# A third buffer for loaded weight units paid for with two 4 KB tiles, and three joining copies queued behind the last weight cast

## The chip, the core and the metric

The kernel runs on one core of a Trainium2 chip. The metric is the time of one execution on the device in microseconds (us), lower is better. The kernel before takes 910.29 us, the median of three runs (908.7 to 912.39).

A core has engines that work side by side, each with its own queue in which instructions start in order: TensorE (PE in the profile, with its weight loads as PEld), VectorE (DVE), ScalarE (ACT), GpSimd (POOL) and SyncE (SP). SP computes nothing here; its queue issues the DMAs that bring weights from memory. An instruction that waits for a semaphore holds up all that stands behind it in its queue.

## The reference, cut to what matters

Two layers of an encoder on a sequence of 256 tokens with 1024 columns, all in float32:

```
u = rms_norm(h) ;  one projection u @ w_in -> parts of both branches
branch A (gated linear attention), branch B (grouped-query attention)
mixed = sigmoid(gate_A) * A + sigmoid(gate_B) * B
h = h + rms_norm(mixed @ w_out)
gate, up = split(rms_norm(h) @ w_ffn_in)          # FFN, 2 x 2816 columns
h = h + rms_norm((silu(gate) * up) @ w_ffn_out)
h = h + rms_norm(sigmoid(h @ w_ple_gate) * (p @ w_ple_proj))
```

With 256 tokens every weight is used once for two blocks ("halves", `hf` 0 and 1) of 128 tokens, so the whole of the weights, 169.50 MB read from memory in the profile, passes through the core in one execution.

## The kernel before, in words

**Three products for one.** TensorE multiplies operands that are rounded to a shorter float format. To keep float32's precision each operand is held as a high part (the rounded value) and a low part (what the rounding lost), and a product is taken as high x high, high x low and low x high. `split` (line 133) makes both parts: a copy with a cast on ACT gives the high part, a subtraction on DVE the low part. Both are recorded at line 135, for weights and for activations.

**Weight units.** The weights are cut into units of up to 128 x 2112 floats (8448 bytes on each of 128 partitions). `plan` lists them in the order of use. `Stream` carries them: `start` (line 290) takes a buffer of the pool `rawp` (tiles `raw`, two buffers) and issues the load on SP's queue (line 298); `put` takes a pair of tiles `wh` and `wl` from `wp` (four buffers each); `fill` (line 347) traces the two halves of the unit's split, two casts of 128 x 1024 on ACT and two subtractions on DVE, and then calls `load`, which traces the next load. At most `depth` units (3 or 4) are held cast and unused.

**Seven products for eight.** Some blocks of the gate stage and of the FFN (`PAIRS`) go through `seven` (line 711), which forms sums of weight units and of activations, and does with seven products of 128 x 512 x 512 what takes eight otherwise. `step` (line 323) makes the sums of weights on DVE (lines 327, 330, 333, 338: 128 x 2048 each); the units involved are loaded into borrowed `wh` and `wl` buffers (tiles `lent`) and into a large tile (`big`).

**Order of the FFN.** The string `FFN` (line 43) is the order written by hand: `u` is a step of a plain block (`block`), a digit a step of `seven`, `o` a step of the output product for one unit of `w_ffn_out` (`out_step`, whose matmuls are recorded at line 107; those of the other products at line 123), `p` a load of a gain vector. The blocks are finished in the order of `OUT`.

**Turning the hidden values.** After `silu(gate) * up` a tile of hidden values must be transposed. `turned` (line 1580) does it for all but the last pair by DMA: `turn_out` (line 456) lets ACT part the 32-bit words into two planes of 16 bits (lines 461 and 466) and issues a transposing DMA on SP's queue (line 467); some steps later `take_in` (line 470) lets ACT join the planes again (line 474, the "joining copy", 128 x 1024 elements of 16 bits) and splits the result into the tile `hid`, again with ACT and DVE. The gate stage uses the same pair of functions for the gated output of branch A (line 1467). The last pair of the FFN is transposed on TensorE instead.

**How instructions are ordered.** The program is traced once. Then a scheduler plays it through with estimated durations: on each engine it issues the earliest traced instruction whose operands and buffer are ready in that play, and a tile is given a buffer of its pool when one is free. The order it finds is fixed in the engines' queues. `tc.issue_after(ins)` adds an edge: what is traced within it on the engine of `ins` is queued behind `ins`, without waiting for its end. `tc.high_priority` moves instructions ahead in that choice.

**Buffers.** `b4p` holds ten tiles of 4096 bytes per partition (`mid`) for gains, sums, parted planes and other things; `smp` holds small ones, `rstd` (1 column) and `hss` (8 columns) with four buffers each.

The lines that the change touches are the pools (74 and 77), `Stream` (259, 319 to 321, 347 to 354), `take_in` (470 to 478), `row_rstd` (509), `last_norm` (619), `outputs` (1383) and `turned` (1580 to 1595).

Of the kernel before, what the change touches and what calls it, by code (L numbers as in the profile page):

```python
# [43 lines left out]
PLAIN, PAIRS = (4, 5, 10), (2, 6, 8)  # L44
# [17 lines left out]
def trunk_kernel(ctx: ExitStack, tc: tile.TileContext, a: dict, out: bass.AP):  # L62
# [8 lines left out]
    PSUM = bass.MemoryType.PSUM  # L71

    cp = ctx.enter_context(tc.tile_pool(name="cp", bufs=1))
    rawp = ctx.enter_context(tc.tile_pool(name="rawp", bufs=2))
    wp = ctx.enter_context(tc.tile_pool(name="wp", bufs=4))
    bigp = ctx.enter_context(tc.tile_pool(name="bigp", bufs=9))
    b4p = ctx.enter_context(tc.tile_pool(name="b4p", bufs=10))
    smp = ctx.enter_context(tc.tile_pool(name="smp", bufs=4))
    accp = ctx.enter_context(tc.tile_pool(name="accp", bufs=8, space=PSUM))

# [167 lines left out]
    class Stream:  # L248
# [7 lines left out]

        def __init__(self, depth):
            self.depth, self.held, self.room, self.ready, self.open = depth, 0, 0, [], False
            self.loads, self.jobs, self.lend, self.last = [], [], False, {}
            pairs = {}  # L260
            for item in plan:
                if callable(item):
                    x = Load(item)
                    self.loads.append(x)
                    self.jobs.append(lambda x=x: self.plain(x))
                else:
                    units, n = item
                    if n == 1:
                        b11, b12, b21, b22 = units
                        x, z = (Load(b, lambda tag=tag: self.lent(tag), tag == "wh") for b, tag in ((b11, "wh"), (b12, "wl")))  # L270
                        y, q = Load(b22, big), Load(b21)
                        pairs[id(units)] = x, y, z, q
                        self.loads += [x, y, z]
                    if n == 5:
                        self.loads.append(q)
                    self.jobs.append(lambda p=pairs[id(units)], n=n: self.step(n, *p))
# [41 lines left out]

        def made(self, x):
            for piece in self.put(x):  # L320
                split(*piece)

        def step(self, n, x, y, z, q):
            c = slice(0, 2048)
# [22 lines left out]
        def fill(self):  # L347
            while self.open and self.held < self.depth and self.jobs:
                n = self.total - len(self.jobs)
                pieces = self.jobs.pop(0)()  # L350
                for piece in pieces or ():
                    self.last[n] = split(*piece)
                if pieces:
                    self.load()

# [111 lines left out]
        nc.sync.dma_start_transpose(out=words.rearrange("p (x t) -> p x t", t=P), in_=planes)  # L467
        return apart

    def take_in(hi, lo, src, parts, behind=None):  # L470

        tn = hi.shape[-1]
        with tc.issue_after(behind.ins) if behind is not None else nullcontext():
            nc.scalar.copy(
                parts.bitcast(U16).rearrange("p (k t s) -> p k t s", s=2, t=tn),
                src.bitcast(U16).rearrange("p (s k t) -> p k t s", s=2, t=tn),
            )
        split(hi, lo, parts.rearrange("p (k t) -> p k t", t=tn))

    last_pow = [None]  # L480

# [22 lines left out]
    def row_rstd(parts, behind=None):  # L504

        ss, r, junk = small(3, "ss"), small(1, "rstd"), mid() if parts[0].shape[-1] > 512 else t512()
        for j, src in enumerate(parts):  # L510
            n = src.shape[-1]
            if j == 2 and behind is not None:
                last_square[0] = nc.vector.scalar_tensor_tensor(
                    out=junk[:, :n], in0=src, scalar=1.0 / 1024.0, in1=src, op0=ALU.mult, op1=ALU.mult,
                    accum_out=ss[:, j : j + 1],
                )
                nc.vector.tensor_scalar(
                    out=r, in0=ss[:, 2:3], scalar1=ss[:, 0:1], scalar2=None, op0=ALU.add
                )
            else:  # L520
                with tc.issue_after(behind.ins) if j and behind is not None else nullcontext():
                    last_square[0] = nc.scalar.activation(
                        junk[:, :n], src, AF.Square, scale=1.0 / 32.0, accum_out=ss[:, j : j + 1]
                    )
            if len(parts) == 3 and j == 1:

                with in_turn():
                    last_pow[0] = nc.gpsimd.tensor_scalar(
                        out=ss[:, 0:1], in0=ss[:, 0:1], scalar1=ss[:, 1:2], scalar2=EPS if behind is not None else 0.0,
                        op0=ALU.add, op1=ALU.add,  # L530
                    )
        with in_turn():
            if behind is None or len(parts) == 2:
                nc.gpsimd.tensor_scalar(
                    out=r, in0=ss[:, 0:1], scalar1=ss[:, len(parts) - 1 : len(parts)], scalar2=EPS,
                    op0=ALU.add, op1=ALU.add,
                )
        last_pow[0] = nc.gpsimd.tensor_tensor(out=r, in0=r, in1=neghalf[:, 0:1], op=ALU.pow)
        return r
# [76 lines left out]
    def last_norm(parts, g, hf):  # L616

        with tc.high_priority(AHEAD):
            yt, junk, ss, r, c = mid(), mid(), small(3, "ss"), small(1, "rstd"), 0
            cuts = []  # L620
            for src in parts:
                cuts.append(slice(c, c + src.shape[-1]))
                c += src.shape[-1]
            nc.scalar.activation(junk[:, cuts[0]], parts[0], AF.Square, scale=1.0 / 32.0, accum_out=ss[:, 0:1])
            nc.vector.scalar_tensor_tensor(
                out=junk[:, cuts[1]], in0=parts[1], scalar=1.0 / 1024.0, in1=parts[1], op0=ALU.mult, op1=ALU.mult,
                accum_out=ss[:, 1:2],
            )
            with in_turn():
                nc.gpsimd.tensor_scalar(  # L630
                    out=ss[:, 2:3], in0=ss[:, 0:1], scalar1=ss[:, 1:2], scalar2=EPS, op0=ALU.add, op1=ALU.add
                )
            total = nc.vector.tensor_tensor_reduce(
                out=junk[:, cuts[2]], in0=parts[2], in1=parts[2], scale=1.0 / 1024.0, scalar=ss[:, 2:3],
                op0=ALU.mult, op1=ALU.add, accum_out=r,
            )
            nc.gpsimd.tensor_tensor(out=r, in0=r, in1=neghalf[:, 0:1], op=ALU.pow)
            yt = [acc(), yt[:, 0:256], acc()[:, 0:256]]
            for j, (src, c) in enumerate(zip(parts, cuts)):
                with tc.issue_after(total.ins) if j else nullcontext():  # L640
                    vmul(yt[j], src, g[:, c])
            for j, c in enumerate(cuts):
                x = h[:, hf, c]
                if j == 1:
                    nc.scalar.activation(yt[j], yt[j], AF.Copy, bias=0.0, scale=r)
                    nc.gpsimd.tensor_tensor(out=x, in0=yt[j], in1=x, op=ALU.add)
                else:
                    nc.vector.scalar_tensor_tensor(out=x, in0=yt[j], scalar=r, in1=x, op0=ALU.mult, op1=ALU.add)
                (nc.scalar if j == 1 else nc.sync).dma_start(out[0, hf * P : (hf + 1) * P, c], x)
# [397 lines left out]
    for l in range(DEPTH):  # L1047
# [332 lines left out]
        def outputs(hf, pr):  # L1380

            o = aux()
            ss = small(8, "hss")
            for i in range(2):
                hd = 2 * pr + i
                c = slice(hd * 256, (hd + 1) * 256)
                oh = o[:, i * 256 : (i + 1) * 256]
                for s in range(2):

                    idx = hf if s == hf else (2 if s == 0 else 3)  # L1390
                    mm3(oh, [t[:, hd, idx, :] for t in sc], [t[:, s, c] for t in v], s == 0, s == 1)
            for i in range(2):
                c = slice((2 * pr + i) * 256, (2 * pr + i + 1) * 256)
                nc.scalar.activation(
                    on[:, hf, c], o[:, i * 256 : (i + 1) * 256], AF.Square, scale=1.0 / 16.0, accum_out=ss[:, i : i + 1]
                )
            inv_sqrt(ss[:, 0:2], 2, 1.0, EPS, eps_out[hf])
            for i in range(2):
                hd = 2 * pr + i
                scale_gain(  # L1400
                    on[:, hf, hd * 256 : (hd + 1) * 256], o[:, i * 256 : (i + 1) * 256], ss[:, i : i + 1], ggla
                )
# [177 lines left out]
        def turned(src, k, hf):  # L1580

            def turn():
# [3 lines left out]
                else:  # L1586
# [5 lines left out]
                    while (k, hf) == (0, 0) and (0, 1) not in apart:  # L1592
                        yield 1
                    dst = hid.at(k, 2, 0, T) if hf is None else hid.at(k, 4, hf * P, P)
                    take_in(*dst, src, parts, apart[0, 1] if (k, hf) == (0, 0) else None)

            t = Task(turn(), part[0], k // 4)
            for i in range(2) if hf is None else (hf,):
# [190 lines left out]
```

## Time and profile before

| | |
|---|---|
| median of three runs | 910.29 us (908.7 to 912.39) |
| the profiled execution | 908.97 us, its span from first to last instruction 907.2 us |
| mean granted TensorE clock | 0.997 |
| TensorE busy | 896.5 us, 4447 matmuls |
| VectorE busy | 791.2 us |
| ScalarE busy | 635.3 us |
| GpSimd busy | 103.6 us |
| moved by DMA | 180.25 MB, mean 199 GB/s |

"Busy" counts the time in which at least one instruction of the engine runs. A row of a group or of the timeline names line, engine, operation, the tile written `<-` the tiles read, the shape, how many (`x8`), the busy time and the mean time of one. A bracket or the last column tells how long the engine sat idle just before, and what ended that wait. Tile names carry layer and stage: `wl_0ffnin` is a low part of weights cast in the FFN of layer 0, `big_0gg` a tile of the gate stage. A matmul's end is modelled, so one that starts soon after another overlaps it in the record.

### The profile page before, as it was taken

The numbers are of one execution on the slowest core, as the hardware profiler recorded it, in microseconds if no ns is written. First come the engines' busy times: TensorE is split into PE (matmuls) and PEld (weight loads), VectorE is DVE, ScalarE is ACT, GpSimd is POOL, SyncE is SP. The second block draws the span as 40 slices with busy tenths as digits, with TensorE's granted clock in tenths as the row PEclk, the third lists the DMA queues.
The fourth block names the chain that finished last, engine by engine and source line by source line (L and its number), as shares of the span: only waits on it lengthen the run. The fifth ranks groups of instructions, "written<-read, shape, count | busy, mean of one in ns | idle before, by whom it ended". The sixth has DMA issues, their size and how long they took to land.

```text
span 907.2 us, 12121 instructions
## 1 busy us (share of the span) xinstructions
PE 896.5 (99%) x4447; PEld 758.1 (84%) x4447; DVE 791.2 (87%) x1021; ACT 635.3 (70%) x1027; POOL 103.6 (11%) x157
## 2 busy tenths in 40 slices
PE   9999999999999999999999999999999999999997
PEld 8898888878888888877898888888888888888786
DVE  7999989987769989898779899799877799999984
ACT  6688679664569686666676687697645796958563
POOL 3700221300100000000244001110001000000001
PEclk9999999999999999999999999999999999999998
DMA  8654449657497685947575524475574966858461
GB/s 284 219 189 137 140 140 241 212 185 235 139 300 197 211 252 179 285 140 258 183 281 191 182 93 140 139 231 179 193 233 132 312 179 200 249 212 242 144 244 47
DMA packets 116967, 180.25 MB, mean 199 GB/s; under 512 B 30942, under 2 KB 55014, under 8 KB 116396
## 3 DMA queue, kind: packets, MB, share of 16 engines
q1 hardware_dynamic: 116748, 179.35, 61.4%
q8 instruction: 35, 0.57, 0.3%
q14 instruction: 24, 0.20, 0.1%
q10 hardware_dynamic: 160, 0.14, 0.0%
HBM read 169.50 MB, written 3.15 MB: 190 GB/s over the span
## 4 chain that ended last, share of the span: by engine, by line
PE 71%; DVE 14%; DMA 7%; issue 3%; ACT 3%; POOL 0%; POOLq 0%; SPq 0%; ACTq 0%; DVEq 0%
PE acc_1ffnin L123 10%; PE acc_1gate L123 7%; PE acc_0ffnin L123 5%; DVE wl_0ffnin L135 5%; PE acc_1ffnin L107 5%; DVE wl_0gate L135 3%; PE acc_1rq L123 3%; PE acc_0gqk L107 2%; PE acc_1gqk L107 2%; PE acc_1wout L123 2%; PE acc_0ple L123 2%; PE acc_1gg L123 2%; PE acc_1v L123 2%; PE acc_0v L123 2%; PE acc_1merge L123 2%
## 5 line engine op out<-in xcount | busy, mean ns | idle before, releaser
L135 ACT CAST wh_1ffnin<-raw_1ffnin 128x1024 fp32r<-128x1024 f32 x38 | 38.3, 1049 | 21.7 <-DMA raw_1ffnin<-in_w_ffn_out_dram 7.2
L135 DVE TENSOR_TENSOR wl_0ffnin<-raw_0ffnin,wh_0ffnin 128x1024 fp32r<-128x1024 f32 x38 | 44.7, 1221 | 8.5 <-ACT wh_0ffnin L135 8.4
L135 ACT CAST wh_0ffnin<-raw_0ffnin 128x1024 fp32r<-128x1024 f32 x38 | 38.0, 1047 | 19.6 <-DMA raw_0ffnin<-in_w_ffn_out_dram 11.1
L135 DVE TENSOR_TENSOR wl_1ffnin<-raw_1ffnin,wh_1ffnin 128x1024 fp32r<-128x1024 f32 x38 | 44.9, 1220 | 7.6 <-ACT wh_1ffnin L135 7.5
L107 PE MATMUL acc_0ffnin<-wh_0ffnin,big_0ffnin 128*128 128x512 f32 x176 | 45.4, 392 | 0.5 <-DVE big_0ffnin L135 0.5
L107 PE MATMUL acc_1ffnin<-wh_1ffnin,big_1ffnin 128*128 128x512 f32 x176 | 45.2, 390 | 0.0
L123 PE MATMUL acc_1ffnin<-wh_1ffnin,big_1wout 128*128 128x512 f32 x168 | 41.5, 389 | 0.0
L123 PE MATMUL acc_0ffnin<-wh_0ffnin,big_0wout 128*128 128x512 f32 x168 | 41.5, 389 | 0.0
L107 PEld LDWEIGHTS acc_0ffnin<-wh_0ffnin,big_0ffnin 128*128 128x128 f32 x176 | 32.7, 188 | 8.1 <-DVE big_0ffnin L135 0.9
L107 PEld LDWEIGHTS acc_1ffnin<-wh_1ffnin,big_1ffnin 128*128 128x128 f32 x176 | 33.0, 188 | 7.0
L123 PEld LDWEIGHTS acc_1ffnin<-wh_1ffnin,big_1wout 128*128 128x128 f32 x168 | 31.5, 188 | 6.6
L123 PEld LDWEIGHTS acc_0ffnin<-wh_0ffnin,big_0wout 128*128 128x128 f32 x168 | 31.5, 188 | 6.5
L135 DVE TENSOR_TENSOR wl_0ffnin<-lent_0ffnin,wh_0ffnin 128x1024 fp32r<-128x1024 f32 x30 | 35.7, 1220 | 0.6 <-ACT wh_0ffnin L135 0.6
L135 DVE TENSOR_TENSOR wl_1ffnin<-lent_1ffnin,wh_1ffnin 128x1024 fp32r<-128x1024 f32 x30 | 35.6, 1217 | 0.0
L135 ACT CAST wh_1ffnin<-lent_1ffnin 128x1024 fp32r<-128x1024 f32 x30 | 30.3, 1051 | 4.6 <-DVE lent_1ffnin L333 1.5
L135 ACT CAST wh_0ffnin<-lent_0ffnin 128x1024 fp32r<-128x1024 f32 x30 | 30.3, 1050 | 4.4 <-PE acc_0ffnin L123 1.6
L135 DVE TENSOR_TENSOR wl_0gate<-raw_0gate,wh_0gate 128x1024 fp32r<-128x1024 f32 x20 | 24.0, 1246 | 7.9 <-ACT wh_0gate L135 7.9
L135 DVE TENSOR_TENSOR wl_1gate<-raw_1gate,wh_1gate 128x1024 fp32r<-128x1024 f32 x20 | 23.6, 1220 | 7.3 <-ACT wh_1gate L135 7.3
L135 ACT CAST wh_0gate<-raw_0gate 128x1024 fp32r<-128x1024 f32 x20 | 19.8, 1046 | 12.8 <-DMA raw_0gate<-in_w_o_gla_dram 6.7
L135 ACT CAST wh_1gate<-raw_1gate 128x1024 fp32r<-128x1024 f32 x20 | 19.9, 1049 | 11.3 <-DMA raw_1gate<-in_w_o_gla_dram 4.7
L107 PE MATMUL acc_0ffnin<-wl_0ffnin,big_0ffnin 128*128 128x512 f32 x88 | 25.4, 399 | 1.4 <-DVE wl_0ffnin L135 1.4
L107 PE MATMUL acc_1ffnin<-wl_1ffnin,big_1ffnin 128*128 128x512 f32 x88 | 24.5, 395 | 0.6 <-DVE wl_1ffnin L135 0.6
(730 smaller groups left out, 2739.5 us busy)
## 6 DMA issues: line engine op xcount, KB each, us to landing
raw_0ffnin<-in_w_ffn_out_dram SPq DMA_DIRECT2D x11, 1024.0 KB, 6.4
raw_1ffnin<-in_w_ffn_out_dram SPq DMA_DIRECT2D x11, 1024.0 KB, 6.3
lent_0ffnin<-in_w_ffn_in_dram SPq DMA_DIRECT2D x6, 1024.0 KB
lent_1ffnin<-in_w_ffn_in_dram SPq DMA_DIRECT2D x6, 1024.0 KB, 9.0
raw_0v<-in_w_in_dram SPq DMA_DIRECT2D x4, 1024.0 KB, 5.1
raw_0gate<-in_w_o_gla_dram SPq DMA_DIRECT2D x4, 1024.0 KB, 5.9
raw_0gate<-in_w_o_attn_dram SPq DMA_DIRECT2D x4, 1024.0 KB, 5.0
raw_0wout<-in_w_ffn_in_dram SPq DMA_DIRECT2D x8, 512.0 KB, 6.3
```

The lines of the kernel that those rows point to most:

```text
L107: return nc.tensor.matmul(o, lhsT, rhs, start=start, stop=stop)
L123: nc.tensor.matmul(o, x, y, start=start and n == 0, stop=stop and n == len(seq) - 1, **kw)
L135: return nc.scalar.copy(hi, src), nc.vector.tensor_tensor(out=lo, in0=src, in1=hi.bitcast(F32), op=ALU.subtract)
```

## The change

The pool of loaded units gets a third buffer. Its 8448 bytes come from two of the ten `mid` tiles (8192 bytes) and from two of four buffers each of `rstd` and `hss`. `Stream` now remembers in `cast` the last pair of instructions that cast a weight unit's half (the ACT cast and the DVE subtraction). `take_in` takes a sequence of instructions to queue behind, and queues its split behind them too, not the joining copy alone. `turned` passes `ws.cast` for three joins of each layer: that of the first FFN tile's second half (`k` 0, `hf` 1) and both of the second pair (`k` is `2 * PAIRS[1]`, 12). The join of the first tile's first half still comes behind the parting of the second, now with its split.

```diff
-    rawp = ctx.enter_context(tc.tile_pool(name="rawp", bufs=2))
+    rawp = ctx.enter_context(tc.tile_pool(name="rawp", bufs=3))
...
-    b4p = ctx.enter_context(tc.tile_pool(name="b4p", bufs=10))
+    b4p = ctx.enter_context(tc.tile_pool(name="b4p", bufs=8))
...
         def made(self, x):
             for piece in self.put(x):
-                split(*piece)
+                self.cast = split(*piece)
...
                 for piece in pieces or ():
-                    self.last[n] = split(*piece)
+                    self.last[n] = self.cast = split(*piece)
...
-    def take_in(hi, lo, src, parts, behind=None):
+    def take_in(hi, lo, src, parts, behind=()):
         tn = hi.shape[-1]
-        with tc.issue_after(behind.ins) if behind is not None else nullcontext():
+        with ExitStack() as order:
+            for x in behind:
+                order.enter_context(tc.issue_after(x.ins))
             nc.scalar.copy(
...
-        split(hi, lo, parts.rearrange("p (k t) -> p k t", t=tn))
+            split(hi, lo, parts.rearrange("p (k t) -> p k t", t=tn))
...
-        ss, r, junk = small(3, "ss"), small(1, "rstd"), mid() if parts[0].shape[-1] > 512 else t512()
+        ss, r, junk = small(3, "ss"), small(1, "rstd", 2), mid() if parts[0].shape[-1] > 512 else t512()
...
-            ss = small(8, "hss")
+            ss = small(8, "hss", 2)
...
-                    take_in(*dst, src, parts, apart[0, 1] if (k, hf) == (0, 0) else None)
+                    late = (k, hf) == (0, 1) or k == 2 * PAIRS[1]
+                    take_in(*dst, src, parts, ws.cast if late else (apart[0, 1],) if (k, hf) == (0, 0) else ())
```

`last_norm` asks for two buffers of `rstd` in the same way.

More of the change, by code (lines that the diff above doesn't have):

```diff
@@ L258, in __init__ @@
             self.depth, self.held, self.room, self.ready, self.open = depth, 0, 0, [], False
-            self.loads, self.jobs, self.lend, self.last = [], [], False, {}
+            self.loads, self.jobs, self.lend, self.last, self.cast = [], [], False, {}, None
             pairs = {}
@@ L618, in last_norm @@
         with tc.high_priority(AHEAD):
-            yt, junk, ss, r, c = mid(), mid(), small(3, "ss"), small(1, "rstd"), 0
+            yt, junk, ss, r, c = mid(), mid(), small(3, "ss"), small(1, "rstd", 2), 0
             cuts = []
```

## The prediction, made before the result was known

> **What bounds the kernel now.** I read the page's first part, then who waited for whom on TensorE, then the chain.
>
> ```profile
> span 907.2 us, 12121 instructions
> PE 896.5 (99%) x4447; PEld 758.1 (84%) x4447; DVE 791.2 (87%) x1021; ACT 635.3 (70%) x1027; POOL 103.6 (11%) x157
> ```
> ```profile
> PE acc_0ffnin L107 <- DVE wl_0ffnin L135: 1.4, 5, 0.4
> ...
> PE acc_1ffnin L107 <- DVE wl_1ffnin L135: 0.6, 2, 0.4
> PE acc_0ffnin L107 <- DVE big_0ffnin L135: 0.5, 1, 0.5
> PE acc_0gate L123 <- ACT wh_0gate L135: 0.3, 1, 0.3
> PE aux_0merge L450 <- DVE big_0gate L1527: 0.2, 1, 0.2
> ```
>
> TensorE is the bound, and what it still loses is small. Past the warm-up it waited ten times, 1.4 + 0.6 + 0.5 + 0.3 + 0.2 = 3.0 us. The record hides a part of each wait, since the modelled end of a matmul lies behind the place where the next could start:
>
> ```profile
> L123 PE MATMUL acc_0ffnin<-wh_0ffnin,big_0wout 128*128 128x512 f32 x168 | 41.5, 389 | 0.0
> ```
> ```profile
> 781.81 5.44 PE acc_1ffnin L123 x24
> ```
>
> One of 128x512 is recorded as 389 ns, but 24 in a row take 5.44 us, 227 ns each. So a wait shows only what goes beyond 389 - 227 = 162 ns. Ten waits hide 1.6 us: **all that late operands cost past the warm-up is about 4.6 us**. Neither edit touches a matmul, so this is the ceiling of any gain.
>
> **The joins that move.** The timeline of ACT and DVE, end of the FFN, both layers:
>
> ```profile
> 377.96 1.18 ACT L474 COPY mid_0ffnin<-t_0ffnin 128x1024 uint16<-128x1024 uint16 x1 [1.12 <-DMA t_0ffnin<-mid_0ffnin]
> 382.47 1.17 ACT L474 COPY mid_0ffnin<-t_0ffnin 128x1024 uint16<-128x1024 uint16 x1 [2.67 <-DMA t_0ffnin<-mid_0ffnin]
> 383.55 2.00 ACT L135 CAST wh_0ffnin<-raw_0ffnin 128x1024 fp32r<-128x1024 f32 x2
> 384.62 2.36 DVE L135 TENSOR_TENSOR wl_0ffnin<-raw_0ffnin,wh_0ffnin 128x1024 fp32r<-128x1024 f32 x2 [2.23 <-ACT wh_0ffnin L135]
> ...
> 829.98 1.18 ACT L474 COPY mid_1ffnin<-t_1ffnin 128x1024 uint16<-128x1024 uint16 x1 [2.83 <-DMA t_1ffnin<-mid_1ffnin]
> 832.14 2.36 DVE L135 TENSOR_TENSOR wl_1ffnin<-raw_1ffnin,wh_1ffnin 128x1024 fp32r<-128x1024 f32 x2 [1.17 <-ACT wh_1ffnin L135]
> ```
>
> These are the joins of the second pair (k 12). The last one stands at the head of ACT's queue for 2.67 us (2.83 in layer 1) until its transposing DMA lands. Behind it stand the casts of a weight unit, and behind these DVE, idle 2.23 and 1.17 us. Where DVE is then late:
>
> ```profile
> 387.04 0.74 PE L107 MATMUL acc_0ffnin<-wl_0ffnin,big_0ffnin 128*128 128x512 f32 x2 [0.25 <-DVE wl_0ffnin L135]
> 400.74 0.73 PE L107 MATMUL acc_0ffnin<-wl_0ffnin,big_0ffnin 128*128 128x512 f32 x2 [0.26 <-DVE wl_0ffnin L135]
> 401.87 0.73 PE L107 MATMUL acc_0ffnin<-wl_0ffnin,big_0ffnin 128*128 128x512 f32 x2 [0.40 <-DVE wl_0ffnin L135]
> ...
> 848.26 0.73 PE L107 MATMUL acc_1ffnin<-wl_1ffnin,big_1ffnin 128*128 128x512 f32 x2 [0.16 <-DVE wl_1ffnin L135]
> 849.39 0.73 PE L107 MATMUL acc_1ffnin<-wl_1ffnin,big_1ffnin 128*128 128x512 f32 x2 [0.40 <-DVE wl_1ffnin L135]
> ```
>
> With the join behind them, the casts at 383.55 can run in ACT's idle time; two take 2.00 us, and 2.67 (2.83) are free. DVE starts up to 2.23 (1.17) us sooner, more than any one of these waits (at most 0.40 + 0.16). All five go: 0.25 + 0.26 + 0.40 + 0.16 + 0.40 = 1.47 shown, 5 x 0.162 = 0.81 hidden, **2.28 us**. The k 12 join of the first half (377.96) already stands behind the cast traced last before it, so its 1.12 us may stay. The join of the first tile's second half (k 0) waited as well, but no TensorE wait follows it: nothing.
>
> A moved join brings its own split along, a cast and a subtraction, and issues no DMA. For that split TensorE waits in the output step of unit 6, the L107 group that contains the wait at 400.74. The last join moves from 382.47 to about 385, with some 14 us to spare: nothing. If a cast behind which it stands had to wait for a buffer, those 14 us are the cover.
>
> **The third raw buffer.** A load now waits for the buffer of the unit before the one whose casts precede it in the trace.
>
> ```profile
> ACT wh_0ffnin L135 <- DMA raw_0ffnin<-in_w_ffn_out_dram: 11.1, 3, 5.7
> ```
> ```profile
> SPq L298 <- DVE wl_0ffnin L135: 77.3, 19, 9.2
> ```
> ```profile
> 182.52 3.90 ACT L135 CAST wh_0gate<-raw_0gate 128x1024 fp32r<-128x1024 f32 x4 [6.69 <-DMA raw_0gate<-in_w_o_gla_dram]
> 183.62 2.13 PE L123 MATMUL acc_0gate<-wh_0gate,big_0gg 128*128 128x512 f32 x8 [0.25 <-ACT wh_0gate L135]
> 420.67 0.73 PE L107 MATMUL acc_0ffnin<-wl_0ffnin,big_0ffnin 128*128 128x512 f32 x2 [0.26 <-DVE wl_0ffnin L135]
> ```
> ```profile
> 176.00 10.36 SPq L298 DMA_DIRECT2D raw_0gate<-in_w_o_gla_dram  x2
> ```
>
> SP's queue stood for 77.3 us before loads until DVE freed a buffer, and ACT's casts then waited for these loads. At 182.52 ACT had waited 6.69 us for a load issued at 176.00. With the buffer that came free one unit sooner it goes out about a unit's matmuls earlier (24 x 227 ns = 5.4 us), far more than TensorE waited. That wait goes: 0.25 + 0.16 = 0.41. So does the one at 420.67, whose unit can be there earlier: 0.26 + 0.16 = 0.42. Most of ACT's other waits for loads end before TensorE notices: nothing. I leave the remaining three waits (aux_0merge, big_0ffnin, the first on wl_0ffnin): they are not followed back to a load or a moved join, between 0 and 4.6 - 3.1 = 1.5 us together.
>
> **Two mid tiles fewer.** Nine are in use at one place: the gate stage, when the fourth form is split beside three forms, two sums, one spare and two gated halves.
>
> ```profile
> 142.43 0.65 ACT L135 CAST mid_0gate<-t_0gate 128x512 fp32r<-128x512 f32 x1
> ```
> ```profile
> 150.42 0.69 DVE L135 TENSOR_TENSOR mid_0gate<-t_0gate,mid_0gate 128x512 fp32r<-128x512 f32 x1
> ```
>
> That cast moves from 142.43 until DVE has read a sum for the last time, some five us; DVE's own part of the split stood at 150.42 anyway. Cost 0 to 0.65 us per layer, the whole cast without cover. I take 0, since ACT is not the later of the two there (rows below). The gains that lose their early buffer are read long after. `rstd` and `hss`: a norm reads its root before the next can be made; 0.
>
> **The sum.** 2.28 + 0.41 + 0.42 = 3.1 us. Against the profiled execution, 908.97 us (span 907.2 and 1.8 around it): 905.9. The median of the runs is 1.3 higher, 910.29: **907.2 us**.
>
> **Rivals.**
>
> **Transposes behind a third load (slower).** One more load of 1 MB may be in flight when a transposing DMA is issued, and the joins that are not moved wait for it at the head of ACT's queue.
>
> ```profile
> raw_0v<-in_w_in_dram SPq DMA_DIRECT2D x4, 1024.0 KB, 5.1
> ```
> ```profile
> DMA to landing us min/median/max: 3.2/4.0/6.6
> ```
> ```profile
> 145.66 6.09 SPq L467 DMA_TRANSPOSE mid_0gg<-big_0gg  x4
> 153.32 2.25 ACT L474 COPY big_0gg<-mid_0gg 128x1024 uint16<-128x1024 uint16 x2
> 160.57 1.14 ACT L135 CAST big_0gg<-big_0gg 128x512 fp32r<-128x512 f32 x2
> ```
> ```profile
> 162.44 1.28 DVE L135 TENSOR_TENSOR big_0gg<-big_0gg,big_0gg 128x512 fp32r<-128x512 f32 x2
> 164.16 1.98 PE L123 MATMUL acc_0gate<-wh_0gate,big_0gg 128*128 128x512 f32 x8
> ```
> ```profile
>   DMA t_0ffnin<-mid_0ffnin: 6.2, 5
>   DMA t_1ffnin<-mid_1ffnin: 3.2, 2
> ```
>
> The second row is for the transposing DMAs, from issue to landing. Four transposes take 6.09 us to issue, 1.5 each, so the second goes out at 147.2 and lands by the median of 4.0 at 151.2, 2.1 us before its join at 153.32. From there to TensorE the slack is 162.44 - 161.71 = 0.73 on ACT and 164.16 - 163.72 = 0.44 on DVE. A delay d costs d - 3.3 in each layer. In the FFN seven joins waited, three of them not moved and so without slack; by the 2.28 us that 1.12 + 2.67 + 2.83 = 6.62 us of such waits cost, each costs 0.34 d. With d = 5.1, one load: 2 x 1.8 + 3 x 1.7 = 8.8 us, the time is 907.2 + 8.8 = **916.0**. It is slower than before from d = 3.0, where 3 x 0.34 d alone is 3.1 us. For it: 3.2 to 6.6 us to landing says that transposes share with loads. Against it: SP stands less before loads, so a transpose is issued no later.
>
> The Trainium skill ("DMA: Bandwidth & Descriptors", section "Issuing engines are not separate DMA queues") says that all DMAs run on the same 16 engines and interleave, whoever issued them. By that rule each added load slows a transpose beside it, and the time would go towards this rival's; the spread of the landings agrees, but no row here shows three loads at once.
>
> **The buffer does nothing.** If the fixed queue order leaves a load where it was, behind the casts that precede it in the trace, only the joins help: 910.29 - 2.28 = **908.0**. For it: the code still starts a load after a unit's casts. Against it: in the trace of before a load leaves as soon as its buffer is free.
>
> **Everything goes.** DVE is early enough throughout: 910.29 - 4.6 = **905.7**.
>
> **How the numbers follow.** A measurement of this kernel tells about 0.5% from no change, 4.55 us: faster is below 905.7, slower above 914.8. Forecast 0.40, buffer without effect 0.18, everything 0.18, late transposes 0.24. The first two are no change, but for 0.02 of the forecast; the third ends at the bound, and I count 0.16 of it as faster: 0.18 in all. The fourth passes the upper bound from d = 4.7, or sooner if more than three joins are without slack, or if the tiles given up add their 0.65 a layer: 0.18. No change is the rest, 0.64. The range reaches from 904.1 (the third case, less the 1.6 us by which the lowest run lay under the median) to 914.0 (the fourth at three quarters of its price).
>
> **What would show it.** Right: no idle before the last L474 copy of each FFN that holds back casts, no wait on wl_0ffnin near 387 and 400 and on wl_1ffnin near 848, ACT's waits for raw_0ffnin well under 11.1 us, TensorE busy unchanged. Wrong: new waits of TensorE on big_0gg or in the FFN ahead of which an L474 copy waits for a transpose; or loads issued no sooner.

## The result, and the profile after

| | before | after |
|---|---|---|
| median of 8 runs each | 910.32 us (906.48 to 912.39) | 905.56 us (904.91 to 908.41) |
| span of the profiled execution | 907.2 us | 903.5 us |

The ratio is 0.9962 with a 95% interval of 0.9946 to 0.9979, a gain of 3.5 us (1.9 to 4.9). It is estimated over all runs and is not the ratio of the two medians, which differ by 4.8 us; the gains below are worked out from such ratios and intervals too. The page of the changed kernel and what TensorE waited for (total, times, longest, in us):

```profile
span 903.5 us, 12157 instructions
PE 894.6 (99%) x4447; PEld 759.9 (84%) x4447; DVE 790.9 (88%) x1021; ACT 634.5 (70%) x1027; POOL 105.4 (12%) x157
```
```profile
PE warm L107 <- POOL seed L144: 1.0, 1, 1.0
PE aux_1wout L450 <- DVE mid_1wout L544: 0.4, 1, 0.4
PE acc_0gqk L107 <- DVE mid_0at L135: 0.2, 1, 0.2
```

None of the ten waits of before is in this list, the three that the prediction left included. Two small ones elsewhere are left: 0.4 + 0.2 and twice the 162 ns that a record hides, 0.9 us, against 4.6 before. The difference, 3.7 us, is that of the spans of these two executions, 907.2 - 903.5. No wait for a late operand in the FFN is left in the list.

Where the join stood in front of the casts, the timeline of ACT at the end of both FFNs now reads:

```profile
380.24 2.01 ACT L135 CAST wh_0ffnin<-raw_0ffnin 128x1024 fp32r<-128x1024 f32 x2 [1.46 <-PE acc_0ffnin L107]
382.14 1.16 ACT L476 COPY mid_0ffnin<-t_0ffnin 128x1024 uint16<-128x1024 uint16 x1
...
825.27 2.01 ACT L135 CAST wh_1ffnin<-raw_1ffnin 128x1024 fp32r<-128x1024 f32 x2 [1.67 <-PE acc_1ffnin L107]
827.18 1.17 ACT L476 COPY mid_1ffnin<-t_1ffnin 128x1024 uint16<-128x1024 uint16 x1
```

The casts run first, 3.3 us sooner than the 383.55 of before. Neither copy has a bracket: the last join of each FFN no longer waits. And the casts themselves now wait for TensorE, which has to read an old `wh` before it can be overwritten: the weights are as early as their buffers allow. The groups of the FFN's casts and subtractions show the same over the whole stage (the last column is the idle time before them, and what ended it), first of before, then of after:

```profile
L135 ACT CAST wh_1ffnin<-raw_1ffnin 128x1024 fp32r<-128x1024 f32 x38 | 38.3, 1049 | 21.7 <-DMA raw_1ffnin<-in_w_ffn_out_dram 7.2
L135 ACT CAST wh_0ffnin<-raw_0ffnin 128x1024 fp32r<-128x1024 f32 x38 | 38.0, 1047 | 19.6 <-DMA raw_0ffnin<-in_w_ffn_out_dram 11.1
L135 DVE TENSOR_TENSOR wl_1ffnin<-raw_1ffnin,wh_1ffnin 128x1024 fp32r<-128x1024 f32 x38 | 44.9, 1220 | 7.6 <-ACT wh_1ffnin L135 7.5
L135 DVE TENSOR_TENSOR wl_0ffnin<-raw_0ffnin,wh_0ffnin 128x1024 fp32r<-128x1024 f32 x38 | 44.7, 1221 | 8.5 <-ACT wh_0ffnin L135 8.4
```
```profile
L135 DVE TENSOR_TENSOR wl_1ffnin<-raw_1ffnin,wh_1ffnin 128x1024 fp32r<-128x1024 f32 x38 | 45.0, 1221 | 2.8 <-ACT wh_1ffnin L135 2.7
L135 DVE TENSOR_TENSOR wl_0ffnin<-raw_0ffnin,wh_0ffnin 128x1024 fp32r<-128x1024 f32 x38 | 44.9, 1221 | 4.0 <-ACT wh_0ffnin L135 4.0
L135 ACT CAST wh_1ffnin<-raw_1ffnin 128x1024 fp32r<-128x1024 f32 x38 | 38.7, 1051 | 20.8 <-PE acc_1ffnin L107 11.1 <-PE acc_1ffnin L123 5.2 <-DVE wl_1ffnin L135 3.7
L135 ACT CAST wh_0ffnin<-raw_0ffnin 128x1024 fp32r<-128x1024 f32 x38 | 38.5, 1049 | 19.4 <-PE acc_0ffnin L107 9.3 <-PE acc_0ffnin L123 4.8 <-DVE wl_0ffnin L135 4.4
```

DVE's wait for a cast fell to less than half. ACT is nearly as idle before its casts as it was (20.8 and 19.4 us against 21.7 and 19.6), but what ends most of its idle time is now TensorE, not a load. That is how an idle engine looks when it is ahead.

### The profile page after: what moved, and what is told of

It reads as the page before. It is cut to its first block, busy times and chain, and to the rows that moved or that the text cites. A ratio compares the mean times of both kernels' runs of the same rounds, so it can differ in the third digit from the quotient of the medians.

```text
span 903.5 us, 12157 instructions
## 1 busy us (share of the span) xinstructions
PE 894.6 (99%) x4447; PEld 759.9 (84%) x4447; DVE 790.9 (88%) x1021; ACT 634.5 (70%) x1027; POOL 105.4 (12%) x157
## 4 chain that ended last, share of the span: by engine, by line
PE 86%; DVE 6%; ACT 3%; issue 3%; POOL 1%; DMA 1%; POOLq 0%; ACTq 0%; DVEq 0%
PE acc_0ffnin L123 12%; PE acc_1ffnin L123 11%; PE acc_1gate L123 7%; PE acc_1ffnin L107 7%; PE acc_0ffnin L107 7%; PE acc_1rq L123 3%; PE acc_1gqk L107 2%; PE acc_0wout L123 2%; PE acc_0ple L123 2%; PE acc_1gg L123 2%; PE acc_1v L123 2%; PE acc_0v L123 2%; PE acc_1merge L123 2%; PE acc_0merge L123 2%; PE acc_1ple L123 2%
## 5 line engine op out<-in xcount | busy, mean ns | idle before, releaser
L135 ACT CAST wh_1ffnin<-raw_1ffnin 128x1024 fp32r<-128x1024 f32 x38 | 38.7, 1051 | 20.8 <-PE acc_1ffnin L107 11.1
L135 ACT CAST wh_0ffnin<-raw_0ffnin 128x1024 fp32r<-128x1024 f32 x38 | 38.5, 1049 | 19.4 <-PE acc_0ffnin L107 9.3
```

What stands on the lines that cost most here:

```text
L135: return nc.scalar.copy(hi, src), nc.vector.tensor_tensor(out=lo, in0=src, in1=hi.bitcast(F32), op=ALU.subtract)
```

## The experiments

The theory to test was the prediction's: the moved joins are worth 2.3 us, the third buffer 0.8, the tiles given up nothing, and these add up. Against it: the transposes behind a third load; the buffer without effect; the buffer alone doing everything, as a cushion that lets DVE run ahead; and an accident of the order, since every edit makes the scheduler find another one.

**The joins alone**, the changed kernel with the old pools:

```diff
-    rawp = ctx.enter_context(tc.tile_pool(name="rawp", bufs=3))
+    rawp = ctx.enter_context(tc.tile_pool(name="rawp", bufs=2))
...
-    b4p = ctx.enter_context(tc.tile_pool(name="b4p", bufs=8))
+    b4p = ctx.enter_context(tc.tile_pool(name="b4p", bufs=10))
```

(`rstd` and `hss` too have four buffers again.)

> The three joins (and the splits behind them) move as in the change; the pools stay as before (two raw buffers, ten mid tiles). The prediction's theory (joins and buffer cure different waits): the five waits of TensorE on wl_0ffnin near 387 and 400 and on wl_1ffnin near 848 go, 2.3 us less than before; the waits near 183 and 420 stay. The rival, cushion (the third buffer lets DVE run ahead, and with that lead a join's wait reaches TensorE no longer; the joins add nothing of their own): about the same 2.3 us here, since without a lead the join's wait is what makes DVE late. The rival, order (the gain is an accident of the order that the scheduler finds with other pools): no gain, within 1 us of before.

Measured: 907.8 us (12 runs) against 909.22 for the kernel before on the same chip, ratio 0.9968 [0.9949, 0.9987]: 2.9 us less (1.2 to 4.6). TensorE's waits:

```profile
PE acc_1ffnin L107 <- DVE wl_1ffnin L135: 1.4, 2, 1.0
...
PE aux_1ffnout L450 <- DVE h L611: 0.7, 1, 0.7
PE aux_1wout L450 <- DVE mid_1wout L544: 0.5, 1, 0.5
PE aux_0merge L450 <- DVE big_0gate L1529: 0.4, 1, 0.4
PE acc_0rq L107 <- ACT wh_start L144: 0.4, 1, 0.4
```

The five waits near 387, 400 and 848 are gone, as the prediction has it. The two near 183 and 420, which were to stay, are not in the list either (near 183 the cast still stood 6.47 us for its load, and TensorE's wait for it fell below what the list shows). But other waits stand in their place. The six past the warm-up make 3.4 us, and with 6 x 0.162 hidden 4.4, against 4.6 before. The profiled span is 1.3 us less than before, 905.9, and the medians differ by 1.4. So moving the joins mends the named waits; how much time it is worth alone is not settled between 1.2 and 4.6 us.

The 1.4 us on `wl_1ffnin` are new, at another place (785.79 and 786.93) than the two waits that were there. What ACT waited for ahead of it:

```profile
771.94 1.05 ACT L135 CAST wh_1ffnin<-lent_1ffnin 128x1024 fp32r<-128x1024 f32 x1 [3.07 <-DMA lent_1ffnin<-in_w_ffn_in_dram]
```

A cast had to wait for its load, and DVE behind it. That this set the later wait is read off the timeline, not tested. Where no join is late any more, the next late thing here is a load.

**The third buffer alone**, the kernel before with the new pools and the old `take_in`:

```diff
-    rawp = ctx.enter_context(tc.tile_pool(name="rawp", bufs=2))
+    rawp = ctx.enter_context(tc.tile_pool(name="rawp", bufs=3))
...
-    b4p = ctx.enter_context(tc.tile_pool(name="b4p", bufs=10))
+    b4p = ctx.enter_context(tc.tile_pool(name="b4p", bufs=8))
```

(`rstd` and `hss` with two buffers, as in the change.)

> Three raw buffers, eight mid tiles, two buffers of rstd and hss, but every join queued as before. The prediction's theory: 0.8 us less than before; the waits near 183 and 420 go, those near 387, 400 and 848 stay, with ACT idle 2.7 us before the last L474 join of each FFN. Cushion: 3 to 4 us less than before, all waits of TensorE on wl_0ffnin and wl_1ffnin gone though ACT still stands before the join. If the joins with a third load in flight wait longer for their transposes than before: slower than before, with new TensorE waits behind L474, and this is why the joins had to move.

Measured: 905.58 us (12 runs) against 909.22, ratio 0.9956 [0.9938, 0.9974]: 4.0 us less (2.4 to 5.6), all that the whole change brings. Its TensorE has no wait in the FFN either:

```profile
...
PE aux_1wout L450 <- DVE mid_1wout L542: 0.4, 1, 0.4
PE acc_0rq L107 <- ACT wh_start L144: 0.2, 1, 0.2
PE acc_0gqk L107 <- DVE mid_0at L135: 0.2, 1, 0.2
```

The joins of the second pair are where they always were, ahead of the casts, and yet do not wait:

```profile
376.24 2.25 ACT L474 COPY mid_0ffnin<-t_0ffnin 128x1024 uint16<-128x1024 uint16 x2
379.66 2.01 ACT L135 CAST wh_0ffnin<-raw_0ffnin 128x1024 fp32r<-128x1024 f32 x2
```

SP's queue, ahead of them, shows what is different. First the kernel before, then the third buffer alone, around the transposes of the second pair:

```profile
371.52 1.24 SPq L467 DMA_TRANSPOSE t_0ffnin<-mid_0ffnin  x1
372.87 0.57 SPq L298 DMA_DIRECT2D raw_0ffnin<-in_w_ffn_in_dram  x1
374.96 2.21 SPq L467 DMA_TRANSPOSE t_0ffnin<-mid_0ffnin  x1
```
```profile
367.36 0.37 SPq L298 DMA_DIRECT2D raw_0ffnin<-in_w_ffn_in_dram  x1
370.58 4.30 SPq L467 DMA_TRANSPOSE t_0ffnin<-mid_0ffnin  x2
```

With two buffers a weight load was issued between the two transposes, 2.1 us before the second. The join behind that one, at 382.47, began 7.5 us after its transpose was issued, and had waited for it. With three buffers the load left 5.5 us earlier, ahead of both, and the second join began without a wait some 3.7 us after its transpose (issued at about 373.65, the end of the row less the 1.23 us of one; joined at about 377.3). In layer 1 the same load moved from 822.14 to 812.49, the first transpose only from 820.79 to 816.29, and the last join began 6.4 us after its transpose before and 3.6 with the third buffer. The joins-alone kernel still has the load between the transposes, at 372.42.

So these transposes landed sooner, and the buffer mends the late joins of the second pair too. But that is not all that it does. Another join of the same kernel waits longer than any of before, and in front of the casts of a unit:

```profile
317.69 1.17 ACT L474 COPY mid_0ffnin<-t_0ffnin 128x1024 uint16<-128x1024 uint16 x1 [3.98 <-DMA t_0ffnin<-mid_0ffnin]
318.76 2.00 ACT L135 CAST wh_0ffnin<-raw_0ffnin 128x1024 fp32r<-128x1024 f32 x2
```

DVE then sits idle for 2.89 us until the first of these casts, longer than the 2.23 us that made TensorE wait in the kernel before, and still TensorE waits for nothing in the FFN: the weights are far enough ahead to cover it. That is the cushion of the expectation. Which of the two cures the five waits of the second pair, the earlier landing or the cushion, the runs do not separate. Either way the two edits remove the same waits.

**The tiles given up, alone**: the kernel before with only the price paid, eight `mid` tiles and two buffers each of `rstd` and `hss`, and still two raw buffers.

```diff
-    b4p = ctx.enter_context(tc.tile_pool(name="b4p", bufs=10))
+    b4p = ctx.enter_context(tc.tile_pool(name="b4p", bufs=8))
```

> Only the price of the third buffer: eight mid tiles instead of ten, two buffers of rstd and hss, two raw buffers, joins as before. The prediction's theory: nothing, within 0.5 us of before; at most 0.65 us a layer, 1.3 us slower. Order: up to 3 us faster or slower, with the waits of TensorE elsewhere than before.

Measured: 920.78 us (6 runs) against 909.22, ratio 1.0115 [1.0088, 1.0143]: **10.5 us more** (8.0 to 13.0). Most of it is one wait of TensorE, and the cast that it waits for stood 15.55 us for a load:

```profile
PE acc_0gate L123 <- ACT wh_0gate L135: 9.1, 1, 9.1
```
```profile
191.49 3.89 ACT L135 CAST wh_0gate<-raw_0gate 128x1024 fp32r<-128x1024 f32 x4 [15.55 <-DMA raw_0gate<-in_w_o_gla_dram]
```

The two issues of SP's queue around 184 us, what had ended its wait ahead of them, and GpSimd at the same time:

```profile
183.34 0.33 SPq L373 DMA_DIRECT2D mid_0wout<-in_g_ffn_pre_dram  x1
...
184.25 11.08 SPq L298 DMA_DIRECT2D raw_0gate<-in_w_o_gla_dram  x2
```
```profile
SPq L373 <- POOL rope_0merge L812: 10.0, 1, 10.0
```
```profile
179.12 4.20 POOL L812 TENSOR_TENSOR rope_0merge<-mid_0merge 128x64 f32<-128x64 f32 x4
```

The load of the gain `g_ffn_pre` was given the `mid` tile from which GpSimd makes the next layer's rope tables. GpSimd finished with it at 183.32, and the gain's DMA left at 183.34. In the kernel before it found a free tile and left at once:

```profile
169.24 0.43 SPq L373 DMA_DIRECT2D mid_0wout<-in_g_ffn_pre_dram  x1
```

Nobody needed the gain early. But behind it in the queue stood the weight load, which before left at 176.00 and now at 184.25.

**The same with the rope tables made later.** If that is the cause, it must go when the tables take their tile after the gains have theirs. The experiment above, with the call moved behind the output projection (layer 0 only, since only a next layer needs tables):

```diff
-        if l + 1 < DEPTH:
-            ropes = rope_tables(l + 1)
...
         part[0] = f"{l}wout"
...
             kept = keep_embedding()
+        if l + 1 < DEPTH:
+            ropes = rope_tables(l + 1)
```

> As the kernel with only the tiles given up (eight mid tiles, two raw buffers, joins as before), but the rotary tables of the next layer are made after the output projection of layer 0, not before it. Theory, blocked queue: with eight tiles the load of the gain vector g_ffn_pre gets the mid tile of the rotary tables, stands at the head of SP's queue until GpSimd has read that tile, and the weight load behind it goes out 8 us too late; with the tables later it gets a tile that TensorE frees sooner, and the 11 us that the given-up tiles cost go, all but 1 or 2 us: 909 to 912 us. Rival, too few tiles (nine are needed at once in the gate stage, and something waits for the ninth): still 8 us or more slower than before.

Measured: 910.04 us (12 runs) against 910.1, ratio 1.001 [0.9985, 1.0034]. The 10.5 us are gone, with the tiles still given up:

```profile
167.59 0.36 SPq L373 DMA_DIRECT2D mid_0wout<-in_g_ffn_pre_dram  x1
...
176.12 10.17 SPq L298 DMA_DIRECT2D raw_0gate<-in_w_o_gla_dram  x2
```

The weight load is back at 176.12. Given up in this order, the tiles cost nothing that can be measured.

**The changed kernel with every late join moved.** Here all joins of the FFN but the first come behind the last cast:

```diff
-                    late = (k, hf) == (0, 1) or k == 2 * PAIRS[1]
+                    late = (k, hf) != (0, 0)
```

> The change, but all joins of the FFN except the very first come behind the last weight cast, not three of a layer. The prediction's theory: the joins that stay in place wait for nothing that TensorE notices, so the same time as the change within 0.7 us, 3 to 5 us less than before. If a join behind a cast comes too late for its output step: slower than the change by up to 2 us, with TensorE waits on big_0ffnin and big_1ffnin at L107.

Measured: 905.56 us (12 runs) against 909.22, ratio 0.9957 [0.9939, 0.9975]. The joins' waits shrink, and the time is that of the third buffer alone, 905.58. Joins of this kernel, then of the third buffer alone, and what they waited for:

```profile
  DMA t_0ffnin<-mid_0ffnin: 0.2, 1
```
```profile
  DMA t_0ffnin<-mid_0ffnin: 5.0, 3
  DMA t_1ffnin<-mid_1ffnin: 3.8, 2
```

8.8 us of join waits or 0.2, and no difference in time: with the third buffer the late joins that are left cost nothing that can be measured.

**The changed kernel with the rope tables later**, the same move as above, since the changed kernel has the block too. Its SP queue and what ended the wait:

```profile
186.51 0.33 SPq L373 DMA_DIRECT2D mid_0wout<-in_g_ffn_pre_dram  x1
187.41 0.42 SPq L298 DMA_DIRECT2D raw_0gate<-in_w_o_gla_dram  x1
```
```profile
SPq L373 <- POOL rope_0merge L814: 11.5, 1, 11.5
```

> The change, with the rotary tables of the next layer made after the output projection of layer 0. Blocked queue: in the changed kernel the same load stands as long, but a third loaded unit lies ahead of it, so only TensorE's wait near 195 (0.3 us) is left of it; it goes, and the time is the change's within 0.5 us. If the block cost the changed kernel more than that, by the DMA traffic that it bunches behind it: 1 to 2 us less than the change. If two loads fewer ahead of the gate stage's transposes matter: slower.

Measured: 904.98 us (6 runs, 904.76 to 905.97) against 910.1, ratio 0.9948 [0.9932, 0.9963]: 4.7 us less (3.4 to 6.2). The load behind the gain leaves 9.5 us sooner:

```profile
168.98 0.38 SPq L373 DMA_DIRECT2D mid_0wout<-in_g_ffn_pre_dram  x1
177.88 0.38 SPq L298 DMA_DIRECT2D raw_0gate<-in_w_o_gla_dram  x1
```

It is the best version measured, by median, but its interval overlaps that of the change: 11.5 us of blocked queue cost the changed kernel less than can be told. In that kernel the unit cast at 182.52 before had already been loaded (issued at 167.39, not 176.00), so a filled buffer stood between the block and TensorE.

The accident of the order is not excluded by any single run, but four kernels with three raw buffers, in four orders, lie within 904.98 and 905.58, and those with two between 907.8 and 920.78.

## Why the prediction was right, and which steps of it were not

**The time** was forecast at 907.2 us and is 905.56; the profiled one at 905.9 and is 905.28. 3.1 us of gain were forecast, and 3.5 (1.9 to 4.9) measured. That the two agree is in good part luck: two terms were wrong in opposite ways, as the next paragraphs show. (The range has a small slip: three quarters of 8.8 us on 907.2 is 913.8, not 914.0.)

**The ceiling of 4.6 us** fits: the waits gone make 3.7 us, the difference of the spans of one execution each, and the largest gain of any kernel, 4.7 (3.4 to 6.2) in the last one, agrees with it. TensorE's busy time fell by 1.9 us without an instruction less; the hidden parts of the eight waits fewer, 1.3 us, had been counted as busy. That fits the hidden part being added. It also means that one sign named for being right, "TensorE busy unchanged", contradicts the prediction's own count; the other signs came as named.

**The moved joins, 2.28 us:** right in the mechanism, since alone they remove the five named waits. The size is inside the interval (2.9, 1.2 to 4.6), but the trace does not bear it out: new waits took nearly the whole of it. And in the change they bring nothing that can be measured, 905.56 us against 905.58 without them.

**The third buffer, 0.83 us:** too small as a term. Alone it brings 4.0 (2.4 to 5.6). The prediction asked which waits end at a load, and counted two. It did not ask what a lead of one unit does for DVE when a join is late, nor what the earlier load no longer stands in front of: the transposes.

**The sum** 2.28 + 0.41 + 0.42 took the two edits as adding up. They do not: the buffer alone takes 905.58 us, and with the joins moved, three or all but one in each layer, it is 905.56. Alone they bring 2.9 and 4.0, and 6.9 would be more than late operands cost in all. The sum came near the result by luck: the waits that it gave to the joins go with the buffer, and the three waits "left" (up to 1.5 us) went too.

**"Two mid tiles fewer: nothing" is the step that failed.** It looked for who would read the tiles late, and found a cast of 0.65 us and gains that "are read long after". The cast did move, from 142.43 to 150.38 in the kernel with only the tiles given up, eight us and not five, and DVE's part, which was to stay, from 150.42 to 151.66; TensorE has no wait there. But that was beside the point. A DMA that waits for its tile holds SP's queue, and the next weight load stands behind it. Price without cover 10.5 us, with the third buffer below what can be measured. The third buffer, for which the tiles were given up, is also what hides their price.

**The rivals.** "Transposes behind a third load" had something right and the sign wrong. The profile has a landing time for few of the 26 transposes, six in the kernel before (its row 3.2/4.0/6.6 holds no more, and none of the second pair) and three in the changed one. In all eight traces, those issued at least 3.7 us behind a weight load landed within 4.2 us; those issued closer behind one took 3.1 to 6.6, ten of thirteen more than 4.2. So a load just ahead of a transpose does go with a late landing; the third buffer takes such a load away from the second pair. The Trainium skill's rule on this ("DMA: Bandwidth & Descriptors", section "Issuing engines are not separate DMA queues"), that DMAs interleave on the same engines, fits these landings; that a third buffer would make it worse was the prediction's own inference, and it fell. So did the price of a wait for a join: one left in place in the changed kernel waited 3.9 us, longer than any before, and no wait of TensorE in the FFN followed. What stays open: that the load just ahead is the cause of the late landing is read off the traces, and no run changed this alone. "The buffer does nothing" is refuted by the second experiment. "Everything goes", 905.7, describes what happened best, and the prediction gave it 0.18.

## What to carry to other kernels

When a buffer is taken from a pool, ask not only who reads the tile late but what queues behind the DMA that must wait for it: a gain that nobody needed yet held back a weight unit that TensorE needed next. Parts of a change that mend the same waits do not add up, so each part needs a run of its own, and the sum of terms must be held against the total of the waits. A spare buffer in front of the bound engine can pay in places where one does not look for it: here it let DVE run ahead, so that late joins no longer reached TensorE, and it moved a load away from the transposes that shared its queue.

## What the runs showed that was not expected

After TensorE's pause of 9 us in the kernel with only the tiles given up, the granted clock was down (us, TensorE busy with its count, granted clock, DMA share, GB/s):

```profile
183.00:192.00 9.00, 0.47 (x3) 0.71 0.59 204
192.00:194.00 2.00, 1.41 (x3) 0.50 0.00 0
194.00:196.00 2.00, 2.00 (x6) 0.50 0.00 1
196.00:198.00 2.00, 2.00 (x8) 0.75 0.69 259
198.00:200.00 2.00, 2.00 (x11) 1.00 0.96 327
```

0.71 over the first stretch means half clock for its last 5.2 us (1 - 0.5 x 5.2 / 9), from 186.8 on. TensorE's last work before the pause ended at 183.47. From 192.59 to about 197 TensorE worked at half clock and lost some 2.2 us more. With the 9.1 shown and 0.16 hidden this makes 11.5 us, the difference to the span of the kernel with the tables later, 919.2 - 907.7. The Trainium skill ("TensorE: Matmul & The Clock Gate", Part 1 on the clock gate) says that the clock halves after an idle window of about 3.4 us and comes back after about as much work; here it fell some 3.3 us into the pause, and was back about 4.4 us after work began. With the ten short waits of before, 0.5 us at most each, the mean granted clock was 0.997, against 0.993 in all six runs here. So this long wait cost more than its length.
